# Hybrid decoder layer: the second pair of the up-projection in plain fp32, B11's rounding in small steps, and the last chunk's weights split slab by slab

## The chip, the core and the metric

The kernel runs on one core of a Trainium2 chip. TensorE (PE) multiplies, VectorE (DVE) and ScalarE (ACT) prepare its operands and empty its PSUM banks, GpSimd (POOL) adds and issues some DMAs, SyncE (SP) issues the others. The metric is the device time of one execution, in microseconds (us), the median of 3 runs. The engines do not share a program: each runs its own queue in order and waits on semaphores of the others.

## What is computed

One inference step of a decoder layer, for a prompt of 512 tokens and 8 single sample tokens (520 columns). After three groups of mixing heads and their output projection comes the part that the change touches:

```python
def conv_ffn(h, w_up, conv_w, conv_b, w_down, prefix):
    u = jnp.matmul(h, w_up)                       # 2048 -> 2 * 5632
    up = jnp.concatenate([prefix, u], axis=1)
    c = conv_b
    for j in range(CONV_W):                       # causal depthwise, width 3
        c = c + conv_w[j] * up[:, j:j + T]
    gate, val = jnp.split(c, 2, axis=-1)
    y = jnp.matmul(jax.nn.gelu(gate) * val, w_down)   # 5632 -> 2048
...
x = x + jnp.matmul(mix, w_out)
y, conv_new = conv_ffn(rms_norm(x, norm2), w_up, conv_w, conv_b, w_down, conv_buf)
x = x + y                                         # then the final rms_norm
```

All inputs and outputs are fp32.

## The kernel before

**Two ways to multiply.** A *split* product cuts each operand into a rounded part (hi, `F32R`) and a remainder (lo) and adds hi·hi, hi·lo and lo·hi: three matmuls for each 128 rows. A weight split is one rounding on ScalarE (L935) and one subtraction on VectorE (L937); an activation split (`split_act`, L1320 and L1321) is two halves of each. A *plain* product feeds fp32 operands to TensorE as they are, and needs no split.

**Seven products.** The up-projection runs in 44 pairs of 128 output columns: chunk by chunk of 512, gate and value in turn. A pair is a 2 x 2 block product over two halves of the inner dimension and two halves of the 520 columns. Pair 0 (`as_is_units`, L1189) computes it with eight plain block products. Each later pair (`seven_units`) uses seven products of sums of blocks: activations b11, t1 to t4, b21, b22 are sums and differences of the normed activation's four blocks, weights s1 to s4 (`sum1` to `sum4`, L1056 to L1065) are sums of the slab's blocks. Each product is a *unit*; they add into five PSUM banks. `post7` reads the bank that t1's product is in (c22, L1132), and the unit b22 then adds onto that bank; `c12` (L1126) reads the result. The down-projection of the first eight chunks follows in two *groups* of eight pairs each, the first of them plain, the rest with seven products; chunks 8 to 10 are then multiplied by 256 columns at a time with plain splitting (`plain`, L973).

**What is plain so far.** In pair 1, the first pair with seven products, b11, b21 and b22 are plain (`mm_raw`, L1225) and t1 to t4 are split, in the order b11, t1, t2, t3, b21, t4, b22. In pair 2, and in the first two such pairs of each group, b11 alone is plain; from then on b11 is split too, by `prep_b11`: the rounding of the whole block on ScalarE (L1361), two remainders on VectorE (L1365), their two roundings on ScalarE (L1369). It is written ahead of pair 2's sixth unit, in a group ahead of the fourth unit of the second such pair (U2).

**What sets the order.** Units stand in one list. For unit k the program first writes the weight split of unit k + 2, then the steps in `pre` (loads, sums, activation splits), then the matmuls, then `post` (evacuations), then one step of each background generator in `bg` (convolution, loads). The split tiles hi and lo have three buffers each. Engines run what they get in this order.

**Activations of the second norm.** `prep_t1` to `prep_t4` build the normed blocks and their differences and split each right away, during pair 0 and pair 1. Operands live in 14 numbered slots (`slot`), several of which hold first the residual x, which is stored to `x2d` at the start of pair 0, and xg, which pair 0 reads.

**Last chunk.** Chunk 10 is multiplied in 13 slabs of 512 x 256 weights: three for all columns, then twice five for half of the columns. Each slab is two units of 128 columns, each with its own weight split. A finished pair's `finish` squares and scales it on ScalarE (L1545, L1548), adds squares on GpSimd (L1546), transposes on TensorE (L1561) and copies on both (L1564); evacuation is L1479 on VectorE.

Of the kernel before, what the change touches and what calls it, by code (L numbers as in the profile page):

```python
# [17 lines left out]
P = 128  # L18
# [50 lines left out]
def hybrid_step(ctx: ExitStack, tc: tile.TileContext, I: dict, C: dict, O: dict):  # L69
# [862 lines left out]
    def split(view):  # L932
        nk = view.shape[1]
        hi = wp.tile([P, nk, P], F32R, tag="hi", name="hi", bufs=3)
        S.activation(hi, view, AF.Copy)  # L935
        lo = wp.tile([P, nk, P], F32R, tag="lo", name="lo", bufs=3)
        V.tensor_tensor(lo, view, hi.bitcast(F32), op=ALU.subtract)  # L937
        return hi, lo

    class Unit:  # L940


        def __init__(self, prod, mm, post=None):
            self.prod, self.mm, self.pre, self.post, self.w = prod, mm, [], post, None
# [6 lines left out]
    def plain(pairs_, src, act, load_at, cuts_of, evac, post):  # L951

        raws = {}
# [6 lines left out]
        def one(i, j):  # L960
# [17 lines left out]
            u = Unit(lambda: split(raws[i][:, :, j * P:(j + 1) * P]), mm, (lambda: post(i)) if j else None)  # L978
# [223 lines left out]
    def seven_units(p):  # L1202
# [55 lines left out]
        U = {4: Unit(lambda: split(A(p, 1, 1)), mm_split(4, "t4", True), post4),  # L1258
             5: Unit(lambda: split(SS[p, 1]), mm_split(3, "t1", True)),
             6: Unit(lambda: split(SS[p, 2]), mm_split(2, "t2", True), post6),  # L1260
             7: Unit(lambda: split(SS[p, 3]), mm_split(0, "t3", True), post7)}
# [392 lines left out]
```

## Time and profile before

| | us |
|---|---|
| median of 3 runs (lowest, highest) | 2308.23 (2307.58, 2309.12) |
| the profiled execution, its own time | 2307.24 |
| its span | 2305.2 |
| TensorE busy | 2255.0 (98%) |
| VectorE busy | 1591.7 (69%) |
| ScalarE busy | 955.0 (41%) |
| GpSimd busy | 200.9 (9%) |

The mean granted TensorE clock is 0.99 of full speed. The span is what lies between the first and the last instruction on the chip; the execution's own time is 2.0 us longer. Busy TensorE is matmuls with modelled ends. In rows, one plain matmul in the program is two records. The up-projection's pair 0 begins at 858 us, pair 1 at 888, the first group at 1780, the second at 1957, the last chunk at 2228.

### The profile page before, as it was taken

The numbers are of one execution on the slowest core, as the hardware profiler recorded it, in microseconds if no ns is written. First come the engines' busy times: TensorE is split into PE (matmuls) and PEld (weight loads), VectorE is DVE, ScalarE is ACT, GpSimd is POOL, SyncE is SP. The second block draws the span as 40 slices with busy tenths as digits, with TensorE's granted clock in tenths as the row PEclk, the third lists the DMA queues.
The fourth block names the chain that finished last, engine by engine and source line by source line (L and its number), as shares of the span: only waits on it lengthen the run. The fifth ranks groups of instructions, "written<-read, shape, count | busy, mean of one in ns | idle before, by whom it ended". The sixth has DMA issues, their size and how long they took to land.

```text
span 2305.2 us, 42433 instructions
## 1 busy us (share of the span) xinstructions
PE 2255.0 (98%) x18084; PEld 2221.7 (96%) x18084; DVE 1591.7 (69%) x2125; ACT 955.0 (41%) x1345; POOL 200.9 (9%) x424
## 2 busy tenths in 40 slices
PE   8999999999999999899999999999999999999996
PEld 8999999999999998899999999999999999999996
DVE  4365655444553448888888888988887977877446
ACT  6233332323342343544454454445444433434225
POOL 0001021121010110000000000000001001000002
PEclk9999999999999999999999999999999999999998
DMA  5323233334242442343433433343345446445514
GB/s 186 104 83 95 78 99 94 92 112 142 65 147 83 150 147 75 101 126 107 129 118 104 129 119 121 111 129 113 109 130 185 154 138 219 153 129 193 194 56 138
DMA packets 355020, 285.73 MB, mean 124 GB/s; under 512 B 9196, under 2 KB 336712, under 8 KB 353760
## 3 DMA queue, kind: packets, MB, share of 16 engines
q1 hardware_dynamic: 335728, 216.82, 31.2%
q0 software_dynamic: 19104, 66.21, 7.9%
q8 instruction: 142, 2.33, 0.4%
q14 instruction: 46, 0.38, 0.0%
HBM read 248.77 MB, written 36.64 MB: 124 GB/s over the span
## 4 chain that ended last, share of the span: by engine, by line
PE 71%; DVE 4%; ACT 1%; issue 1%; DMA 0%; ACTq 0%; DVEq 0%; POOLq 0%
PE pw L1218 16%; PE pw L1217 16%; PE pw L1219 16%; PE pw L973 9%; PE pg L186 3%; PE pg L190 3%; PE pg L188 3%; PE pw L1189 3%; DVE lo L937 1%; PE pw L1225 1%; ACT hi L935 1%; PE psc L703 1%; PE pob L685 1%; DVE n L1312 0%; PE px L750 0%
## 5 line engine op out<-in xcount | busy, mean ns | idle before, releaser
L935 ACT ACTIVATE hi<-r 128x1024 fp32r<-128x1024 f32 (+1 forms) x222 | 222.8, 1009 | 288.7 <-PE pw L1218 187.0
L937 DVE TENSOR_TENSOR lo<-s,hi 128x1024 fp32r<-128x1024 f32 x227 | 277.7, 1223 | 91.8 <-ACT hi L935 88.1
L935 ACT ACTIVATE hi<-s 128x1024 fp32r<-128x1024 f32 x227 | 240.0, 1058 | 187.0 <-PE pw L1218 174.4
L937 DVE TENSOR_TENSOR lo<-r,hi 128x1024 fp32r<-128x1024 f32 (+1 forms) x222 | 267.1, 1204 | 48.3 <-ACT hi L935 48.3
L186 PE MATMUL pg<-x1h,hi 128*128 128x260 f32 x1408 | 289.9, 287 | 3.0 <-ACT hi L157 1.7
L190 PE MATMUL pg<-x1h,lo 128*128 128x260 f32 x1408 | 284.4, 284 | 0.5 <-DVE lo L159 0.5
L188 PE MATMUL pg<-x1l,hi 128*128 128x260 f32 x1408 | 283.4, 283 | 0.0
L159 DVE TENSOR_TENSOR lo<-raw,hi 128x1024 fp32r<-128x1024 f32 x104 | 127.2, 1223 | 168.6 <-ACT hi L157 156.9
L186 PEld LDWEIGHTS pg<-x1h,hi 128*128 128x128 f32 x1408 | 217.8, 189 | 4.3 <-ACT hi L157 2.0
L190 PEld LDWEIGHTS pg<-x1h,lo 128*128 128x128 f32 x1408 | 217.5, 189 | 0.7 <-DVE lo L159 0.7
L188 PEld LDWEIGHTS pg<-x1l,hi 128*128 128x128 f32 x1408 | 217.1, 189 | 0.0
L1082 DVE SCALAR_TENSOR_TENSOR cv<-u,convc,cv 128x512 f32<-128x512 f32 (+1 forms) x176 | 132.2, 752 | 43.6 <-ACT cv L1077 43.6
L1217 PE MATMUL pw<-b22h,hi 128*128 128x260 f32 x448 | 129.1, 288 | 9.9 <-DVE cv L1145 7.8
L1217 PE MATMUL pw<-t1h,hi 128*128 128x260 f32 x456 | 130.2, 286 | 2.3 <-ACT hi L935 2.3
L1217 PE MATMUL pw<-t3h,hi 128*128 128x260 f32 x456 | 130.1, 285 | 2.3 <-ACT hi L935 2.3
L1219 PE MATMUL pw<-t3h,lo 128*128 128x260 f32 x456 | 130.1, 285 | 0.6 <-DVE lo L937 0.6
L1219 PE MATMUL pw<-t1h,lo 128*128 128x260 f32 x456 | 129.8, 285 | 0.7 <-DVE lo L937 0.7
L1217 PE MATMUL pw<-t4h,hi 128*128 128x260 f32 x456 | 130.3, 286 | 0.0
L1218 PE MATMUL pw<-t3l,hi 128*128 128x260 f32 x456 | 129.7, 284 | 0.0
L1219 PE MATMUL pw<-t4h,lo 128*128 128x260 f32 x456 | 129.1, 283 | 0.5 <-DVE lo L937 0.5
L1219 PE MATMUL pw<-t2h,lo 128*128 128x260 f32 x456 | 128.9, 283 | 0.6 <-DVE lo L937 0.6
L1218 PE MATMUL pw<-t1l,hi 128*128 128x260 f32 x456 | 129.4, 284 | 0.0
(442 smaller groups left out, 6357.1 us busy)
## 6 DMA issues: line engine op xcount, KB each, us to landing
r<-in_w_up SPq DMA_DIRECT2D x88, 1024.0 KB, 5.3
raw<-in_w_in SPq DMA_DIRECT2D x88, 512.0 KB, 3.6
r<-in_w_down SPq DMA_DIRECT2D x40, 1024.0 KB, 5.8
agd<-cv POOLq DMA_DIRECT2D x16, 520.0 KB, 3.7
g<-agd POOLq DMA_DIRECT2D x8, 1040.0 KB, 10.6
cv<-x2d POOLq DMA_DIRECT2D x16, 520.0 KB, 6.7
x2d<-cv POOLq DMA_DIRECT2D x16, 520.0 KB, 6.1
raw<-in_w_out SPq DMA_DIRECT2D x16, 512.0 KB, 3.3
```

The costliest lines, as they stand in the source:

```text
L159: V.tensor_tensor(lo, raw, hi.bitcast(F32), op=ALU.subtract)
L186: PE.matmul(ps[:, i, 0:b - a], wh, xh[:, a:b], start=first, stop=False)
L188: PE.matmul(ps[:, i, 0:b - a], wh, xl[:, a:b], start=False, stop=False)
L190: PE.matmul(ps[:, i, 0:b - a], wl, xh[:, a:b], start=False, stop=last)
L935: S.activation(hi, view, AF.Copy)
L937: V.tensor_tensor(lo, view, hi.bitcast(F32), op=ALU.subtract)
L973: PE.matmul(ps[t][:, 0:b - a], wt[:, kk], x[:, a:b], start=kk == 0 and wt is hi and x is xh, stop=kk == nk - 1 and wt is lo)
L1082: V.scalar_tensor_tensor(cv[:, j, 0:w], u[:, j, i:i + w], convc[:, i, n], cv[:, j, 0:w], op0=ALU.mult, op1=ALU.add)
L1189: PE.matmul(ps, A(p, n, i)[:, m], x[:, m], start=i == 0 and m == 0, stop=i == 1 and m == 7, skip_group_check=True)
L1217: PE.matmul(ps(k), hi[:, m], xh[:, m], start=a, stop=False, skip_group_check=True)
L1218: PE.matmul(ps(k), hi[:, m], xl[:, m], start=False, stop=False, skip_group_check=True)
L1219: PE.matmul(ps(k), lo[:, m], xh[:, m], start=False, stop=z, skip_group_check=True)
```

## The change

**Pair 1 wholly plain.** All seven units of pair 1 use `mm_raw`, in the order of the other pairs (b11, t4, t1, t2, t3, b21, b22), and no weight of pair 1 is split. Its second slab's successor is loaded from the third unit on.

**Activation splits put off.** Norms and differences come first, during pair 0, each block in a slot of its own; the splits of t1 and t2 come at the end of pair 0, of t3, t4 and b21 during pair 1, of b22 at the start of pair 2. Slots are renumbered for that.

**B11 in small steps.** `prep_b11` becomes a background generator of six steps, one behind each unit: rounding of each half, remainder of each half, rounding of each remainder. It starts ahead of pair 2's second unit, in a group ahead of U2's first.

**Last chunk.** A slab of the last chunk is split once, both units' columns in one instruction on each engine, and four units ahead instead of two.

```diff
-            u = Unit(lambda: split(raws[i][:, :, j * P:(j + 1) * P]), mm, (lambda: post(i)) if j else None)
+            def prod():
+                if not both:
+                    return split(raws[i][:, :, j * P:(j + 1) * P])
+                if j == 0:
+                    pieces[i] = split(raws[i])
+                return tuple(t[:, :, j * P:(j + 1) * P] for t in pieces[i])
+
+            u = Unit(prod, mm, (lambda: post(i)) if j else None)
+            u.ahead = 4 if both else 2
...
-        if p - 1 in as_is or p - 2 in as_is:
-            U[1] = Unit(None, mm_raw(1, lambda: A(p, 0, 0), (1, 1), True), post1)
-        else:
-            U[1] = Unit(lambda: split(A(p, 0, 0)), mm_split(1, "b11", True), post1)
-        if first:
-            U[2] = Unit(None, mm_raw(1, lambda: A(p, 0, 1), (2, 1), False), post2)
-            U[3] = Unit(None, mm_raw(3, lambda: SS[p, 2], (2, 2), False), post3)
-        else:
-            U[2] = Unit(lambda: split(A(p, 0, 1)), mm_split(1, "b21", False), post2)
-            U[3] = Unit(lambda: split(SS[p, 2]), mm_split(3, "b22", False), post3)
-        seq = (1, 5, 6, 7, 2, 4, 3) if first else (1, 4, 5, 6, 7, 2, 3)
-        at = [U[n] for n in seq]
-        at[3 if first else 2].pre.append(lambda: sum4(p))
+        def unit(k):
+            w, fresh = weights[k], k not in (2, 3)
+            if first or (k == 1 and p - 2 in as_is) or (k == 1 and p - 1 in as_is):
+                return Unit(None, mm_raw(banks[k], w, names[k], fresh), posts.get(k))
+            return Unit(lambda: split(w()), mm_split(banks[k], names[k], fresh), posts.get(k))
+
+        at = [unit(k) for k in (1, 4, 5, 6, 7, 2, 3)]
+        at[4 if first else 2].pre.append(lambda: sum4(p))
-            if first:
-                at[4].pre.append(lambda: load_pair(nx, 1))
-                at[6].pre.append(lambda: (sum1(nx), sum3(nx)))
-            else:
-                at[0].pre.append(lambda: load_pair(nx, 1))
-            if not first and nx not in as_is:
-                at[3].pre.append(lambda: sum1(nx))
-                at[4].pre.append(lambda: sum3(nx))
-                at[5].pre.append(lambda: sum2(nx))
+            at[2 if first else 0].pre.append(lambda: load_pair(nx, 1))
+            if nx not in as_is:
+                at[5 if first else 3].pre.append(lambda: sum1(nx))
+                at[6 if first else 4].pre.append(lambda: sum3(nx))
+                if not first:
+                    at[5].pre.append(lambda: sum2(nx))
...
     def prep_t1():
         norm2()
         B[1, 2] = normed(0, 1, 12)
-        B[1, 1] = normed(0, 0, 13)
-        B["t"] = slot(0, "t12", F32)
-        diff(B["t"], B[1, 2], B[1, 1])
-        xop["t1"] = split_act(B["t"], 1, 2, "t1")
+        B["b11"] = B[1, 1] = normed(0, 0, 13)
+        B["t1"] = slot(0, "t1", F32)
+        diff(B["t1"], B[1, 2], B[1, 1])
 
     def prep_t2():
-        B[2, 2] = normed(1, 1, 3)
-        diff(B["t"], B[2, 2], B["t"])
-        xop["t2"] = split_act(B["t"], 4, 5, "t2")
+        B["b22"] = normed(1, 1, 3)
+        B["t2"] = slot(1, "t2", F32)
+        diff(B["t2"], B["b22"], B["t1"])
+
+    def prep_t4():
+        B["b21"] = normed(1, 0, 2)
+        B["t4"] = slot(4, "t4", F32)
+        diff(B["t4"], B["t2"], B["b21"])
 
     def prep_t3():
-        diff(B[1, 2], B[2, 2], B[1, 2])
-        xop["t3"] = split_act(B[1, 2], 6, 7, "t3")
-
-    def prep_t4():
-        diff(B["t"], B["t"], B[2, 1])
-        xop["t4"] = split_act(B["t"], 9, 12, "t4")
+        B["t3"] = B[1, 2]
+        diff(B["t3"], B["b22"], B["t3"])
+
+    def split_b(name, h, l):
+        xop[name] = split_act(B[name], h, l, name)
 
     def prep_b11(h_, l_, tag, bufs):
 
         hi = slot(h_, "b11h")
-        S.activation(hi, B[1, 1], AF.Copy)
+        for a in (0, 4):
+            S.activation(hi[:, a:a + 4], B[1, 1][:, a:a + 4], AF.Copy)
+            yield
         halves = []
         for a in (0, 4):
             h = ff.tile([P, 4, HALF], F32R, tag=tag, name="b11x", bufs=bufs)
             V.tensor_tensor(h, B[1, 1][:, a:a + 4], hi[:, a:a + 4].bitcast(F32), op=ALU.subtract)
             halves.append(h)
+            yield
         lo = slot(l_, "b11l")
         for a, h in zip((0, 4), halves):
             S.activation(lo[:, a:a + 4], h.bitcast(F32), AF.Copy)
-        xop["b11"] = hi, lo
-
-    def split_b(i, t, name, h, l):
-        xop[name] = split_act(B[i, t], h, l, name)
-
-    def prep_n21():
-        B[2, 1] = normed(1, 0, 8)
+            xop["b11"] = hi, lo
+            yield
+
+    places = {"b11": (3, 13), "t4": (11, 0), "t1": (5, 6), "t2": (7, 8), "t3": (9, 10), "b21": (1, 12), "b22": (4, 2)}
+
+    def split_p(name, of=places):
+        split_b(name, *of[name])
 
     N, U1, U2 = ups[:3]
     N[0].pre.append(prep0)
     N[1].pre.append(prep_t1)
-    N[4].pre.append(prep_t2)
+    N[2].pre.append(prep_t2)
+    N[3].pre.append(prep_t4)
+    N[4].pre.append(prep_t3)
     N[5].pre += [lambda: sum1(1), lambda: sum2(1)]
-    U1[0].pre += [prep_t3, lambda: sum3(1)]
-    U1[2].pre += [prep_n21, prep_t4]
-    U1[6].pre.append(lambda: split_b(2, 1, "b21", 10, 11))
-    U2[0].pre.append(lambda: split_b(2, 2, "b22", 8, 0))
-    U2[5].pre.append(lambda: prep_b11(3, 13, "cv", 3))
+    N[6].pre += [lambda: sum3(1), lambda: split_p("t1")]
+    N[7].pre.append(lambda: split_p("t2"))
+    for k, u, name in ((0, U1, "t3"), (3, U1, "t4"), (5, U1, "b21"), (0, U2, "b22")):
+        u[k].pre.append(lambda name=name: split_p(name))
+    U2[1].pre.append(lambda: bg.append(prep_b11(3, 13, "cv", 3)))
...
-        U1[0].pre.append(lambda: split_b(2, 1, "b21", *new["b21"]))
-        U1[1].pre.append(lambda: split_b(2, 2, "b22", *new["b22"]))
-        U2[3].pre.append(lambda: prep_b11(*new["b11"], "u", 2))
+        U1[0].pre.append(lambda: split_b("b21", *new["b21"]))
+        U1[1].pre.append(lambda: split_b("b22", *new["b22"]))
+        U2[0].pre.append(lambda: bg.append(prep_b11(*new["b11"], "u", 2)))
...
+    made = 0
     for k, u in enumerate(units):
-        if k + 2 < len(units) and units[k + 2].prod:
-            units[k + 2].w = units[k + 2].prod()
+        while made < min(k + u.ahead + 1, len(units)):
+            if units[made].prod:
+                units[made].w = units[made].prod()
+            made += 1
```

Where B11's rounding stands on ScalarE. At the end of pair 2, before; b11h and b11l are its rounded part and its rounded remainder, b11x the remainder, r and s slabs and sums of weights, q the running sum, and L1077 the first tap of pair 2's convolution:

```order
L935 ACTIVATE hi<-r_9307 128x1024
L935 ACTIVATE hi<-s_9506 128x1024
L935 ACTIVATE hi<-r_9508 128x1024
L1361 ACTIVATE b11h<-n_9198 128x2080
L1369 ACTIVATE b11l<-b11x 128x1040 x2
L1123 COPY u<-pw_9518 128x260
L935 ACTIVATE hi<-r_9510 128x1024
L1077 ACTIVATE cv<-u,convc 128x512 x2
```

And after the change, at the same place on ScalarE:

```order
L934 ACTIVATE hi<-s_9428 128x1024
L1364 ACTIVATE b11h<-n_9198 128x1040
L934 ACTIVATE hi<-s_9407 128x1024
L1364 ACTIVATE b11h<-n_9198 128x1040
L934 ACTIVATE hi<-r_9310 128x1024
L934 ACTIVATE hi<-s_9428 128x1024
L934 ACTIVATE hi<-r_9430 128x1024
L1133 COPY u<-pw_9440 128x260
L1374 ACTIVATE b11l<-b11x 128x1040
L934 ACTIVATE hi<-r_9432 128x1024
L1087 ACTIVATE cv<-u,convc 128x512 x2
L1374 ACTIVATE b11l<-b11x 128x1040
```

The two halves of b11h moved ahead by two weight roundings and more, and the second half of b11l moved behind the convolution's first tap.

VectorE in the first group, in U2, before; cv is the residual that the sums are added to, the adds of q_19945 and pw_19847 are c22:

```order
L1065 TENSOR_TENSOR s_19734<-r_19578,s_19734 128x1024
L937 TENSOR_TENSOR lo<-r_19578,hi 128x1024
L1056 TENSOR_TENSOR s_19876<-r_19800 128x1024
L1365 TENSOR_TENSOR b11x<-g_19248,b11h 128x1040 x2
L1231 TENSOR_TENSOR q_19912<-q_19811,pw_19887 128x260
L937 TENSOR_TENSOR lo<-s_19734,hi 128x1024
L1059 TENSOR_TENSOR s_19918<-r_19798,r_19800 128x1024
L1231 TENSOR_TENSOR q_19945<-q_19912,pw_19920 128x260
L1145 TENSOR_TENSOR cv<-cv,q_19945 128x260
L1145 TENSOR_TENSOR cv<-cv,pw_19847 128x260
```

And after the change, at the same place on VectorE:

```order
L1075 TENSOR_TENSOR s_19657<-r_19501,s_19657 128x1024
L1369 TENSOR_TENSOR b11x<-g_19171,b11h 128x1040
L936 TENSOR_TENSOR lo<-r_19501,hi 128x1024
L1066 TENSOR_TENSOR s_19804<-r_19723 128x1024
L1241 TENSOR_TENSOR q_19831<-q_19734,pw_19806 128x260
L1369 TENSOR_TENSOR b11x<-g_19171,b11h 128x1040
L936 TENSOR_TENSOR lo<-s_19657,hi 128x1024
L1069 TENSOR_TENSOR s_19839<-r_19721,r_19723 128x1024
L1241 TENSOR_TENSOR q_19866<-q_19831,pw_19841 128x260
L1155 TENSOR_TENSOR cv<-cv,q_19866 128x260
```

The same instructions stand ahead of c22; one half of the remainder moved ahead of the weight remainder, the other behind q2.

VectorE in the last chunk, one half pair, before; x is the residual that is evacuated to, y the transposed output, u the scaled block:

```order
L937 TENSOR_TENSOR lo<-r_24060,hi 128x512
L1479 TENSOR_TENSOR x_22931<-pw_24171,x_22931 128x256
L937 TENSOR_TENSOR lo<-r_24060,hi 128x512
L1479 TENSOR_TENSOR x_22931<-pw_24189,x_22931 128x256
L1564 COPY y_23799<-py 128x256
L1547 TENSOR_SCALAR u<-x_22931,gv 128x256
```

And after the change:

```order
L936 TENSOR_TENSOR lo<-r_24027,hi 128x1024
L1485 TENSOR_TENSOR x_22856<-pw_24076,x_22856 128x256
L1485 TENSOR_TENSOR x_22856<-pw_24090,x_22856 128x256
L1570 COPY y_23724<-py 128x256
L1553 TENSOR_SCALAR u<-x_22856,gv 128x256
```

Two remainders of 512 became one of 1024, which stands ahead of both evacuations and belongs to a slab one pair further on.

## Rows read from the trace of the kernel before

**Rows 1.** Stretches: start:end, length; PE, PEld, DVE, ACT, POOL busy; clock, DMA share, GB/s.

```profile
858.00:880.00 22.00, 22.00 (x105) 19.13 (x104) 16.16 (x18) 6.33 (x11) 0.00 (x0) 1.00 0.49 150
...
920.00:960.00 40.00, 31.71 (x215) 30.48 (x214) 32.81 (x36) 19.68 (x22) 1.43 (x7) 0.87 0.32 98
...
960.00:1780.00 820.00, 820.00 (x6828) 820.00 (x6827) 721.63 (x829) 397.91 (x474) 54.48 (x185) 1.00 0.41 123
...
2260.00:2290.00 30.00, 25.55 (x200) 23.91 (x200) 22.74 (x52) 18.57 (x40) 7.91 (x6) 1.00 0.32 106
```

**Rows 2.** Chain that ended last: start, us, what.

```profile
788.09 5.79 PE pw L973 x48
...
1809.07 3.51 PE pw L1225 x16
```

**Rows 3.** Timeline, TensorE: start, us, line, out<-in, count, idle before and its releaser.

```profile
888.25 3.67 PE L1225 MATMUL pw<-n,r 128*128 128x260 f32 x16
...
943.24 0.36 PE L1217 MATMUL pw<-b22h,hi 128*128 128x260 f32 x1 [1.85 <-DVE u L1132]
...
950.43 0.38 PE L1217 MATMUL pw<-b11h,hi 128*128 128x260 f32 x1 [2.79 <-ACT u L1123]
...
954.94 0.28 PE L1217 MATMUL pw<-t4h,hi 128*128 128x260 f32 x1
...
1851.65 0.36 PE L1217 MATMUL pw<-b22h,hi 128*128 128x260 f32 x1 [3.92 <-DVE cv L1145]
...
1856.12 0.28 PE L1217 MATMUL pw<-b11h,hi 128*128 128x260 f32 x1
...
2027.75 0.56 PE L1217 MATMUL pw<-b22h,hi 128*128 128x260 f32 x1 [3.92 <-DVE cv L1145]
...
2033.08 0.42 PE L1217 MATMUL pw<-b11h,hi 128*128 128x260 f32 x1
...
2252.07 0.36 PE L973 MATMUL pw<-a10h,hi 128*128 128x256 f32 x1 [0.98 <-DVE x L1479]
```

**Rows 4.** Stretches of TensorE alone: start:end, length, busy (records), clock, DMA share, GB/s.

```profile
1851.60:1856.20 4.60, 4.55 (x25) 0.63 0.00 0
...
2027.70:2033.10 5.40, 5.35 (x25) 0.50 0.00 0
...
2252.10:2256.00 3.90, 3.50 (x29) 1.00 0.42 134
```

**Rows 5.** Timeline, VectorE, pairs 0 and 1.

```profile
867.96 4.70 DVE L1312 TENSOR_TENSOR n<-xg,rbc 128x1040 f32<-128x1040 f32 x4
...
887.64 1.22 DVE L937 TENSOR_TENSOR lo<-s,hi 128x1024 fp32r<-128x1024 f32 x1
```

**Rows 6.** Timeline, ScalarE, pair 2.

```profile
923.70 1.52 ACT L1077 ACTIVATE cv<-u,convc 128x512 f32<-128x512 f32 x2 [4.37 <-DVE u L1126]
...
925.12 1.04 ACT L935 ACTIVATE hi<-s 128x1024 fp32r<-128x1024 f32 x1
```

**Rows 7.** Timeline, VectorE, first group, U2.

```profile
1837.23 1.23 DVE L937 TENSOR_TENSOR lo<-s,hi 128x1024 fp32r<-128x1024 f32 x1 [1.26 <-ACT hi L935]
...
1847.89 1.23 DVE L937 TENSOR_TENSOR lo<-s,hi 128x1024 fp32r<-128x1024 f32 x1 [2.78 <-ACT hi L935]
```

**Rows 8.** Timeline, last chunk, one half pair on three engines; then TensorE's last pair.

```profile
2256.86 0.64 ACT L1545 ACTIVATE cv<-x 128x512 f32<-128x512 f32 x1 [0.86 <-DVE x L1479]
...
2257.64 1.29 POOL L1546 TENSOR_TENSOR cv<-cv 128x512 f32<-128x512 f32 x1 [2.68 <-ACT cv L1545]
...
2257.80 1.14 ACT L935 ACTIVATE hi<-r 128x512 fp32r<-128x512 f32 x2
...
2258.45 1.03 DVE L937 TENSOR_TENSOR lo<-r,hi 128x512 fp32r<-128x512 f32 x1 [1.08 <-ACT hi L935]
...
2259.74 0.68 DVE L937 TENSOR_TENSOR lo<-r,hi 128x512 fp32r<-128x512 f32 x1
...
2260.33 0.42 DVE L1479 TENSOR_TENSOR x<-pw,x 128x256 f32<-128x256 f32 x1
...
2285.48 0.36 PE L973 MATMUL pw<-a10h,hi 128*128 128x264 f32 x1 [1.48 <-DVE x L1479]
```

More of the change, by code (lines that the diff above doesn't have):

```diff
@@ L932, in split @@
     def split(view):
-        nk = view.shape[1]
-        hi = wp.tile([P, nk, P], F32R, tag="hi", name="hi", bufs=3)
+        hi = wp.tile(list(view.shape), F32R, tag="hi", name="hi", bufs=3)
         S.activation(hi, view, AF.Copy)
-        lo = wp.tile([P, nk, P], F32R, tag="lo", name="lo", bufs=3)
+        lo = wp.tile(list(view.shape), F32R, tag="lo", name="lo", bufs=3)
         V.tensor_tensor(lo, view, hi.bitcast(F32), op=ALU.subtract)
@@ L943, in __init__ @@
         def __init__(self, prod, mm, post=None):
-            self.prod, self.mm, self.pre, self.post, self.w = prod, mm, [], post, None
+            self.prod, self.mm, self.pre, self.post, self.w, self.ahead = prod, mm, [], post, None, 2
     units = []
@@ L951, in plain @@
     def plain(pairs_, src, act, load_at, cuts_of, evac, post):
-        raws = {}
+        raws, pieces = {}, {}
         def load(i):
@@ L976, in mm @@
                     evac(n0 + j, t, a, b, ps[t][:, 0:b - a])
-            u = Unit(lambda: split(raws[i][:, :, j * P:(j + 1) * P]), mm, (lambda: post(i)) if j else None)
+            both = nk == 4
+            def prod():
[6 more added lines that the diff above has]
+            u.ahead = 4 if both else 2
             if j == 0:
@@ L1242, in post7 @@
             out.c22(st["q3"], ps(3))
-            if not first:
-                out.c21(st["q3"], ps(4))
+            out.c21(st["q3"], ps(4))
         def post2():
             out.c11(ps(1))
-        def post4():
-            if first:
-                out.c21(st["q3"], ps(4))
         def post3():
@@ L1257, in seven_units @@
         nx = p + 1 if p + 1 < len(pairs) else None
[L1258 to L1261, printed above, removed]
-        if p - 1 in as_is or p - 2 in as_is:
-            U[1] = Unit(None, mm_raw(1, lambda: A(p, 0, 0), (1, 1), True), post1)
-        else:
-            U[1] = Unit(lambda: split(A(p, 0, 0)), mm_split(1, "b11", True), post1)
-        if first:
-            U[2] = Unit(None, mm_raw(1, lambda: A(p, 0, 1), (2, 1), False), post2)
-            U[3] = Unit(None, mm_raw(3, lambda: SS[p, 2], (2, 2), False), post3)
-        else:
-            U[2] = Unit(lambda: split(A(p, 0, 1)), mm_split(1, "b21", False), post2)
-            U[3] = Unit(lambda: split(SS[p, 2]), mm_split(3, "b22", False), post3)
-        seq = (1, 5, 6, 7, 2, 4, 3) if first else (1, 4, 5, 6, 7, 2, 3)
-        at = [U[n] for n in seq]
-        at[3 if first else 2].pre.append(lambda: sum4(p))
+        weights = {1: lambda: A(p, 0, 0), 2: lambda: A(p, 0, 1), 3: lambda: SS[p, 2], 4: lambda: A(p, 1, 1),
+                   5: lambda: SS[p, 1], 6: lambda: SS[p, 2], 7: lambda: SS[p, 3]}
+        names = {1: "b11", 2: "b21", 3: "b22", 4: "t4", 5: "t1", 6: "t2", 7: "t3"}
+        banks = {1: 1, 2: 1, 3: 3, 4: 4, 5: 3, 6: 2, 7: 0}
+        posts = {1: post1, 2: post2, 3: post3, 6: post6, 7: post7}
+        def unit(k):
[5 more added lines that the diff above has]
+        at[4 if first else 2].pre.append(lambda: sum4(p))
         if p == 2:
@@ L1394, in hybrid_step @@
     ORDER = ("b11", "t4", "t1", "t2", "t3", "b21", "b22")
-    places = {"b11": (3, 13), "t4": (9, 12), "t1": (1, 2), "t2": (4, 5), "t3": (6, 7), "b21": (10, 11), "b22": (8, 0)}
     def group(g, old):
@@ L1406, in load_b @@
         def load_b(i, t, s):
[L1407 removed]
+            B[i, t] = B[f"b{i}{t}"] = slot(s, f"g{i}{t}", F32)
             nc.gpsimd.dma_start(B[i, t], src[:, i - 1, :, HALF * (t - 1):HALF * t])
@@ L1609, in hybrid_step @@
         load_wo(i)
-    for u in units[:2]:
-        u.w = u.prod()
+    made = 0
     for k, u in enumerate(units):
-        if k + 2 < len(units) and units[k + 2].prod:
-            units[k + 2].w = units[k + 2].prod()
+        while made < min(k + u.ahead + 1, len(units)):
+            if units[made].prod:
+                units[made].w = units[made].prod()
+            made += 1
         for fn in u.pre:
```

2 lines of the change are left out of this document (removed).

## The prediction

> **What bounds the kernel now.** I read the table by stretch first, then the waits of TensorE, then what stands in front of them on VectorE and ScalarE. From 960 to 1780 us TensorE is busy for all 820 us at the full granted clock, and a stretch of plain fp32 matmuls (858 to 880) is also full [rows 1]. So only the places where it stops can give time. These are 920 to 960 (31.7 busy of 40, clock 0.87), one place in each of the two later groups, and the last 30 us of matmuls (25.6 busy) [rows 1]. The waits that matter for the end of the first place are 1.85 us before b22 of pair 2 and 2.79 before b11 of pair 3; each group has one of 3.92, before b22 of its second split pair [rows 3]. A wait also costs afterwards: the unit behind one of 3.92 us runs at 0.63 in the first group and 0.50 in the second, which is the 1.2 GHz level for most or all of it, and takes 4.47 and 5.33 us; after a wait of 0.98 us in the last chunk the clock stays at 1.00 [rows 3, 4].
>
> A split unit is 24 matmuls, half of a row with 48 in 5.79 us: 2.90. A plain unit is 8 matmuls, which the trace shows as 16 records: 3.51 [rows 2].
>
> **1, pairs 1 and 2 of the up-projection.** *On TensorE* pair 1 turns four split units into plain ones: 4 x (3.51 - 2.90) = +2.4 us. From 888.25 [rows 3], where pair 1 begins, pairs 1 and 2 then hold 8 plain and 6 split units, 28.1 + 17.4 = 45.5, so that pair 3 could begin at 933.7 and its second unit, t4, at 936.6, if nothing waited. That t4 begins at 954.94 now [rows 3]. The end of this term is the start of that t4, because from there no wait is left until the groups.
>
> The Trainium skill (FP8 and Floating Point Precision, TensorE Precision Notes) says that true FP32 takes four passes through the array. Against the three of a split matmul that would be 2.90 x 4/3 = 3.87 a unit, an estimate, and +3.9 us for four units; the row has 3.51 and decides, and the forecast would be 1.4 us higher by the page.
>
> *On VectorE* four remainder instructions of the weights of pair 1 go (1.22 us each, 1.13 from start to start [rows 5]), with four roundings on ScalarE; no wait of pair 1 is then for a split. I set the new order against durations. Pitches: half of an operand 1.15 (four take 4.70 to the end of the last [rows 5]), a 1024-wide instruction 1.13, a tap of the convolution 0.67, a 260-wide one 0.34. Differences and norms come first now: 867.96 + 16 halves (18.4) + two evacuations (0.7) = 887.1, then three sums to 890.5, t1's and t2's remainders with an evacuation behind each to 895.8. That last evacuation frees the bank of the third plain unit, which TensorE reaches at 888.25 + 7.0 = 895.3: a wait of about 0.7. Nothing else stops pair 1; its last sum (s4) is ready by 907, and TensorE needs it at 910. Pair 1 ends at 913.5, the plain unit of pair 2 at 917.0, its five split units at 931.5.
>
> The sixth, b22, adds onto the bank that holds t1's product, so it waits until c22 (L1132) has read it; the 1.85 us row is this wait [rows 3]. On VectorE there stand, between pair 1's last evacuations of the sums (907.6) and that c22: 6 halves (two each of b21 and b22, one of b11's remainder, and the gate product, which is as wide), 12 instructions of 1024, 4 taps, 3 short ones, c22 itself 0.9, and some 1.8 us in which it waits for ScalarE, whose Identity pair (1.52) stands before s1's rounding (1.04) [rows 6]: 6.9 + 13.6 + 2.7 + 1.0 + 0.9 + 1.8 = 26.9, so 934.5, and about 934.8 with what of the early wait comes through. So **the wait moves here**: b22 waits 3.3 us and then runs mostly at 1.2 GHz, 4.4 us (4.47 and 4.51 are what units behind such waits took [rows 3]), to 939.2. Next is b11's second low half. In the new order it stands on ScalarE behind the Identity pair of pair 2, which waits for c12, which waits for b22: 939.2 + c12 0.6 + 1.45 + 1.05 = 942.4. Pair 3's b11 has done its first 12 matmuls by then and does 12 more: t4 at 944.0. **Gain 954.9 - 944.0 = 10.9.** Bounds: none of these waits, 954.9 - 936.6 = 18.3; both with the longest waits and slowest clocks in the rows (3.92 + 5.33 for b22, 2.79 + 4.51 for b11, from 931.5: 948.1), 6.8.
>
> The DMAs of the next slabs move too: pair 2's second slab is now issued after pair 1's second unit (about 895), since its buffer's last reader comes earlier, and has over ten us until its sum is due at 908. ScalarE's table load and gelu stay where they were; they hide behind plain matmuls, and without that cover cost some 2.4 us once. The renamed slots cost nothing: the x2 stores that read slots 4 to 7 are issued at the start of pair 0, and the splits that reuse these slots come behind pair 0.
>
> **2, B11 in steps, twice in the groups.** Now the whole of b11's rounding (two halves as one instruction) and both low halves (2.04) stand on ScalarE before the rounding of s4, for which VectorE waits until 1847.89, and s3, q3 and c22 come behind [rows 7]. In the new order s4's rounding waits only for a free buffer, that is for t2, which ends at 1841.9. VectorE then goes without a wait from s3's remainder: that starts at 1837.23 [rows 7], 0.5 later with the first b11 step ahead of its rounding. Six of 1024 (6.8), two halves (2.3), q2 0.34, q3 and two adds 1.5: 1837.7 + 10.9 = 1848.6. The unit before b22 ends at 1847.56, so 1.1 us of the 3.92 stay. By the 0.98 us row the clock then holds, b22 ends at 1851.5, and b11 waits for the read of its bank, 3.42 us behind c22, until 1852.0. b11 starts at 1856.12 now: **4.1 us**. The second group has the same order and the same 3.92, but a slower unit behind it (b11 at 2033.08, 5.33 after b22's start at 2027.75): 5.0. **Together 9.1.** Bounds: all gone, 3.92 x 2 + 1.57 + 2.43 = 11.8; half of each wait stays and the clock still falls, 3.9.
>
> **3, last chunk.** One loop sets its pace, not TensorE: evacuation, then on ScalarE square, gain, rounding, then on VectorE remainder, next evacuation. The rows for one half pair: square from 2256.86, gain, two roundings 1.14, remainders 1.03 and 0.68, each with an evacuation of 0.34 to 0.42 [rows 8]; 3.97 us a turn. With one slab at once the second rounding no longer hides behind the first remainder: 0.08 + 0.54 + 0.40 + 1.06 + 1.14 + 0.34 + 0.42 = 3.98. No gain per turn. What is gained is the end: splitting two slabs ahead takes the last split off the last turn, where the last pair now waits until 2285.48 [rows 8]. Its predecessor's first bank can then be read at 2283.2, and behind its four transposes the pair starts at 2283.85: **1.6 us.**
>
> Here GpSimd matters: its add runs 2257.64 to 2258.93, and the remainder that starts at 2258.45 takes 1.03 where the next takes 0.68 [rows 8]. In the new order the remainder starts at 2258.9, as the add ends, so I charge nothing. The Trainium skill (SBUF, State Buffer; Who interferes with whom) says that an instruction of VectorE with two SBUF inputs blocks wholly against one of GpSimd that reads SBUF, the later one until the first has ended. By that rule, the trace agrees: 0.48 us of the add were left and 0.35 were lost. If the share were lost in each of 9 turns all the same, the term would be 1.6 - 9 x 0.35 = -1.5; at best the one 0.98 us wait at its start goes too: 2.6.
>
> **Sum.** 10.9 + 9.1 + 1.6 = 21.6 us. The profiled execution took 2307.24 us (span 2305.2 and 2.0 around it), 1.0 below the median of 2308.23. So 2285.6 for an execution like it, and in terms of the median 2286.6, said as 2287.
>
> **The rivals.**
> - *VectorE catches up* (each wait in 1 and 2 closes): 18.3 + 11.8 + 1.6 = 31.7, 2277. For it: VectorE loses four remainders and most of its waits. Against: c22 has 26 us of work before it with hardly a gap. Chance 0.12.
> - *The waits stay* at the lower bounds of 1 and 2 with nothing from 3: 6.8 + 3.9 = 10.7, 2297.5. For it: every wait over 1.8 us brought a slow unit. Against: by the count only 1.1 us is late in a group. Chance 0.15.
> - *The last chunk's halves were better* (the shared remainder in each turn): 2307.24 - 20.0 + 1.5, 2289.7 by the median. Chance 0.08.
> - *Slower, by the clock*: the new 0.7 us wait before pair 1's third unit drops the clock and it stays at 1.2 GHz. Every us of full-speed work costs another; from some 26 us on (21.6 to undo and 4.6 for 0.2%) the kernel is slower, and if it lasts from 895 to the end of pair 2 (38 us of work) the time is 2287 + 38 = 2325. Against: 0.98 us did not drop it, and after drops the rows show it back within a unit or two. Chance 0.03.
>
> **How the numbers follow.** The forecast has 0.62, alone from 2282 to 2292. A measurement of this kernel can tell about 0.2%, 4.6 us, from no change: faster is under 2303.6. The forecast, the first and the third rival lie there, and most of the second: 0.94. Within 0.2%: the far end of the second, 0.03. Slower: 0.03. The range leaves out about 0.1 on each side, the full first rival and the full second: 2280 to 2296.
>
> **What would show it.** Right: pair 1 as 56 plain matmuls without a wait over 1 us; a wait near 3 us for c22 before b22 of pair 2; one inside b11 of pair 3 for the second low half; waits near 1 us in the groups with the clock at 1.00; the last pair without a wait for a remainder. Wrong: a wait at pair 2's first split unit, a granted clock near 0.5 in pair 1, group waits still near 4 us, or a turn of the last chunk well off 4 us.

## The result, and the profile after

| | before | after |
|---|---|---|
| median, us (lowest, highest) | 2308.06 (2307.58, 2309.68), 6 runs | 2288.89 (2287.90, 2289.58), 6 runs |
| the profiled execution, its own time | 2307.24 | 2289.31 |
| its span | 2305.2 | 2287.5 |
| TensorE busy | 2255.0 (98%) | 2248.2 (98%) |
| VectorE busy | 1591.7 | 1581.8 |
| ScalarE busy | 955.0 | 949.5 |

The ratio is 0.9916 (95% interval 0.9903 to 0.9928): 19.2 us faster by the medians. The forecast was 2287, within 2280 to 2296.

By stretches of the kernel after (columns as in [rows 1]), the stretch that ends pair 2 has 33.7 us of matmuls in 40 where it had 31.7, and its clock is 0.96 where it was 0.87. The stretch from 2240 lies in the last chunk: 27.5 of 30. Earlier by the 17.7 us won in all, the last row there answers to 2242.3 to 2272.3 here, with 26.8 of 30 for its 25.6.

```profile
920.00:960.00 40.00, 33.66 (x263) 33.06 (x262) 34.54 (x40) 19.12 (x21) 1.09 (x5) 0.96 0.30 93
960.00:1780.00 820.00, 820.00 (x6798) 818.92 (x6797) 719.34 (x826) 397.11 (x474) 54.58 (x187) 1.00 0.41 123
2240.00:2270.00 30.00, 27.48 (x218) 26.07 (x219) 20.67 (x47) 18.69 (x35) 8.75 (x7) 1.00 0.29 97
```

TensorE's timeline of the kernel after, the rows that answer to [rows 3] and the two new waits (0.59 in pair 1, 0.92 in chunks 8 and 9):

```profile
896.11 2.24 PE L1235 MATMUL pw<-t,s 128*128 128x260 f32 x9 [0.59 <-DVE u L1130]
...
917.07 0.47 PE L1227 MATMUL pw<-t4h,hi 128*128 128x260 f32 x1
...
935.32 0.36 PE L1227 MATMUL pw<-b22h,hi 128*128 128x260 f32 x1 [2.99 <-DVE u L1142]
...
943.10 0.39 PE L1228 MATMUL pw<-b11l,hi 128*128 128x260 f32 x1 [3.12 <-ACT b11l L1374]
...
948.93 0.28 PE L1227 MATMUL pw<-t1h,hi 128*128 128x260 f32 x1
...
1840.19 0.36 PE L1227 MATMUL pw<-b22h,hi 128*128 128x260 f32 x1 [0.81 <-DVE cv L1155]
...
1843.59 0.36 PE L1227 MATMUL pw<-b11h,hi 128*128 128x260 f32 x1 [0.28 <-DVE cv L1155]
...
2012.24 0.36 PE L1227 MATMUL pw<-b22h,hi 128*128 128x260 f32 x1 [0.81 <-DVE cv L1155]
...
2131.06 0.63 PE L972 MATMUL pw<-a8h,hi 128*128 128x260 f32 x2 [0.92 <-ACT hi L934]
...
2236.23 0.38 PE L972 MATMUL pw<-a10h,hi 128*128 128x256 f32 x1 [1.39 <-DVE x L1485]
...
2267.77 0.37 PE L972 MATMUL pw<-a10h,hi 128*128 128x264 f32 x1
```

Since TensorE is the bound, the start of the same unit in both traces tells how much has been won up to there. Read so, the 17.7 us between the two spans come from these places:

| place | before | after | won so far | this part | forecast |
|---|---|---|---|---|---|
| pair 1, first unit | 888.25 | 888.35 | -0.1 | -0.1 | |
| pair 3, t1 | 957.82 | 948.93 | 8.9 | 9.0 | 10.9 |
| first group, t4 after b11 | 1859.01 | 1846.55 | 12.5 | 3.6 | 4.1 |
| second group, the same | 2036.15 | 2018.61 | 17.5 | 5.1 | 5.0 |
| chunks 8 and 9, to the last chunk's first transpose | 2239.74 | 2223.41 | 16.3 | -1.2 | |
| last chunk's last matmul, its end | 2288.64 | 2270.94 | 17.7 | 1.4 | 1.6 |

So the three terms came to 9.0, 8.7 and 1.4, and 1.2 us were lost where the forecast had nothing. The forecast for this execution was 2285.6, the measured 2289.3.

### The profile page after: what moved, and what is told of

Same layout as the page of the kernel before. It is cut to its first block, busy times and chain, and to the rows that moved or that the text cites. A ratio compares the mean times of both kernels' runs of the same rounds, so it can differ in the third digit from the quotient of the medians.

```text
span 2287.5 us, 42302 instructions
## 1 busy us (share of the span) xinstructions
PE 2248.2 (98%) x18052; PEld 2213.2 (97%) x18052; DVE 1581.8 (69%) x2108; ACT 949.5 (42%) x1331; POOL 200.4 (9%) x424
## 4 chain that ended last, share of the span: by engine, by line
PE 70%; DVE 5%; ACT 1%; issue 1%; DMA 1%; ACTq 0%; DVEq 0%; POOLq 0%
PE pw L1227 15%; PE pw L1228 15%; PE pw L1229 15%; PE pw L972 9%; PE pg L186 3%; PE pg L190 3%; PE pg L188 3%; PE pw L1199 2%; DVE lo L936 1%; PE pw L1235 1%; ACT hi L934 1%; DMA r<-in_w_down 1%; PE psc L703 1%; PE pob L685 1%; DVE t L1325 0%
## 5 line engine op out<-in xcount | busy, mean ns | idle before, releaser
L934 ACT ACTIVATE hi<-r 128x1024 fp32r<-128x1024 f32 x208 | 220.4, 1060 | 282.8 <-PE pw L1228 186.9
L936 DVE TENSOR_TENSOR lo<-r,hi 128x1024 fp32r<-128x1024 f32 x208 | 260.5, 1253 | 44.7 <-ACT hi L934 44.7
L1227 PE MATMUL pw<-b21h,hi 128*128 128x260 f32 x448 | 127.8, 285 | 0.0
L157 ACT ACTIVATE hi<-raw 128x1024 fp32r<-128x1024 f32 x104 | 109.6, 1056 | 43.1 <-PE pg L188 36.6
L1228 PE MATMUL pw<-t2l,hi 128*128 128x260 f32 x448 | 127.0, 283 | 0.0
L1228 PE MATMUL pw<-t4l,hi 128*128 128x260 f32 x448 | 126.9, 283 | 0.0
```

The lines of the kernel that those rows point to most:

```text
L157: S.activation(hi, raw, AF.Copy)
L1227: PE.matmul(ps(k), hi[:, m], xh[:, m], start=a, stop=False, skip_group_check=True)
L1228: PE.matmul(ps(k), hi[:, m], xl[:, m], start=False, stop=False, skip_group_check=True)
```

## Experiments

All medians below stand beside a kernel before of 2308.4 to 2308.8 us on the same chip.

**The kernel after once more** (no edit).

> The changed kernel itself once more. In its first profile pair 4 comes 9.0 us earlier than before, counted from pair 1's start; in four later kernels with the same program up to there it is 9.6, 10.5, 9.6 and 10.5. Theory: the length of pairs 2 and 3 differs from execution to execution, by which unit the low clock falls on and by how often b11 waits; this profile lies between 9.0 and 10.5, the time within 1.5 us of 2288.9. Rival: the first profile is the rule for this program, 9.0 again.

Measured: 2290.0 us (2287.22 to 2290.32), ratio 0.9916. Counted from pair 1's first unit to t2 of pair 3, the kernel before takes 72.48 us and the first profile of after 63.48, which is 9.0 less. This second profile has 61.99, which is 10.5 less. The five other kernels below that are the same up to there have 9.6 (twice) and 10.5 (three times). The difference is where the low clock falls and how long it lasts. In the second profile it falls on b22, right behind its wait, and is over before b11; in the two with 9.6 it lasts through b22 (0.50, 5.3 us) into b11. In the first it spares b22 and falls on t4, behind the next wait. Stretches of TensorE alone (columns as in [rows 4]), the first profile's b22, then its t4, then the second profile's b22:

```profile
935.30:938.30 3.00, 2.98 (x25) 1.00 0.00 0
...
944.80:949.00 4.20, 4.20 (x26) 0.66 0.01 2
```

```profile
936.30:940.70 4.40, 4.35 (x25) 0.67 0.00 0
```

**B11's split in the groups as before.**

```diff
-        U2[0].pre.append(lambda: bg.append(prep_b11(*new["b11"], "u", 2)))
+        U2[3].pre.append(lambda: list(prep_b11(*new["b11"], "u", 2)))
```

> The changed kernel with b11's split in the two groups at one go and in its old place, ahead of the fourth unit of the second split pair. Theory: it is this alone that moved the groups; the waits of 3.9 us before b22 come back with slow units behind them, and the time rises by what the starts of the units show, 3.5 + 5.2 = 8.7: 2297.6. Rival: part of the groups' gain came from work that reached them earlier or in another order from the pairs ahead; then the rise is under 6, below 2295.

Measured: 2298.9 us (2298.04 to 2299.32), 10.0 above after's first median, 8.9 above its second. The waits before b22 are back, at 3.85 (first group) and 3.86 us, and the units behind them last 4.4 and 4.5 us. The theory holds. TensorE in the first group:

```profile
1842.89 0.56 PE L1227 MATMUL pw<-b22h,hi 128*128 128x260 f32 x1 [3.85 <-DVE cv L1155]
```

**B11's split in the groups at one go, at its new place.**

```diff
-        U2[0].pre.append(lambda: bg.append(prep_b11(*new["b11"], "u", 2)))
+        U2[0].pre.append(lambda: list(prep_b11(*new["b11"], "u", 2)))
```

> The changed kernel with all six steps of b11's split in the groups written at once, at the place where the first of them stands now (ahead of the second split pair's first unit). Theory: what gave the groups' 8.7 us is the place, not the small steps; both remainders then stand where VectorE has nothing to do (3.73 us without work behind the plain unit), so the 0.81 and 0.28 us that are left in each group go too: 2288.9 - 2.2 = 2286.7. Rival: the steps matter, because ScalarE now stops for the plain unit's end (b11's remainder overwrites what that unit reads) with the weights' roundings behind it; a wait of TensorE of over 1 us comes in each group: 2291 or more.

Measured: 2286.97 us (2285.98 to 2287.28). TensorE waits nowhere in the first group now, and 0.24 us ahead of b11 in the second. Both remainders stand in VectorE's gap behind the plain unit, and ScalarE's stop for that unit's end held nobody up. What won the groups' 8.7 us is the place and not the small steps. Timelines of the first group, ScalarE and VectorE:

```profile
1825.03 2.04 ACT L1374 ACTIVATE b11l<-b11x 128x1040 fp32r<-128x1040 f32 x2 [4.37 <-DVE b11x L1369]
...
1822.55 2.38 DVE L1369 TENSOR_TENSOR b11x<-g,b11h 128x1040 fp32r<-128x1040 f32 x2
1828.32 2.36 DVE L936 TENSOR_TENSOR lo<-s,hi 128x1024 fp32r<-128x1024 f32 x2 [3.38 <-ACT hi L934]
```

**Pair 1's part alone.**

```diff
-    U2[1].pre.append(lambda: bg.append(prep_b11(3, 13, "cv", 3)))
+    U2[5].pre.append(lambda: list(prep_b11(3, 13, "cv", 3)))
...
-        U2[0].pre.append(lambda: bg.append(prep_b11(*new["b11"], "u", 2)))
+        U2[3].pre.append(lambda: list(prep_b11(*new["b11"], "u", 2)))
...
-                if not both:
+                if True:
...
-            u.ahead = 4 if both else 2
+            u.ahead = 2
```

> Only the change in pair 1 (plain units, splits put off): b11's split in pair 2 and in the groups is at one go in its old place, and the last chunk is split as before. Theory: the 8.9 us by which pair 3's t1 came forward belong to pair 1's part alone; c22 has one remainder less ahead of it (b22 waits 1.8 and not 3.0), and b11's split is late instead: 2308.4 - 8.9 = 2299.5. Rival: the small steps carry a good part of it; b11's split of 6.3 us in a row stands behind c22 and holds b11 of pair 3 up by over 4 us: 2303 or more.

Measured: 2299.34 us (2298.85 to 2302.25), 9.5 under the kernel before. b22 waits 1.80 and b11 2.69, about the 1.85 and 2.79 of [rows 3], with a clock of 0.65 and 0.63 behind them. From pair 1's first unit to t2 of pair 3 it takes 63.23 us, 9.25 less than before, where the seven profiles with the small steps have 9.0 to 10.5. So nearly all of the first term is pair 1's: the small steps in pair 2 traded a shorter wait at b11 for a longer one before b22, and were worth between -0.3 and 1.3 us, as far as one profile of this kernel tells.

```profile
935.46 0.36 PE L1227 MATMUL pw<-b22h,hi 128*128 128x260 f32 x1 [1.80 <-DVE u L1142]
...
942.59 0.39 PE L1227 MATMUL pw<-b11h,hi 128*128 128x260 f32 x1 [2.69 <-ACT u L1133]
```

**B11's last two steps as one, in pair 2.**

```diff
             xop["b11"] = hi, lo
-            yield
+            if a == 4 or not together:
+                yield
```

(`together` is set for pair 2 only.)

> The changed kernel with the last two steps of b11's split in pair 2 made one: both roundings of the remainders stand together on ScalarE, ahead of the convolution's Identity pair. Theory: the 3.12 us wait inside b11 of pair 3 is this place in ScalarE's queue and nothing else, and the slow t4 behind it (4.2 at a clock of 0.66) comes from the wait; both go, t1 of pair 3 starts at 944.1 instead of 948.9, 2284.1. Rival 1: the wait of 2.99 us before b22 drops the clock by itself; then 3.1 is gained, 2285.8. Rival 2: the weight rounding that now stands behind both is late for t4, which waits 1 us instead: 2285.1 at best.

Measured: 2286.53 us (2285.26 to 2289.93). The wait inside b11 is gone: both halves of b11l stand ahead of the Identity pair. But the rounding of t1's weights now stands behind that pair too, and t1, begun at 944.27 (expected 944.1), waits 0.75 inside the unit for the remainder made from it and ends 4.1 us after its start, at a clock of 1.00. This is the second rival, one unit later than it said. In this execution a wait of 2.96 before b22 did not lower the clock at all, so it cannot tell how much of the slow t4 came from which wait. ScalarE, then TensorE, then TensorE's stretch that holds t1:

```profile
936.95 2.04 ACT L1374 ACTIVATE b11l<-b11x 128x1040 fp32r<-128x1040 f32 x2 [3.97 <-DVE b11x L1369]
...
941.70 1.52 ACT L1087 ACTIVATE cv<-u,convc 128x512 f32<-128x512 f32 x2 [1.76 <-DVE u L1136]
943.13 1.04 ACT L934 ACTIVATE hi<-s 128x1024 fp32r<-128x1024 f32 x1
...
945.48 0.40 PE L1229 MATMUL pw<-t1h,lo 128*128 128x260 f32 x1 [0.75 <-DVE lo L936]
```

```profile
944.40:948.30 3.90, 3.15 (x26) 1.00 0.43 129
```

**The same, and pair 1's gate product behind c22.**

```diff
+        if p == 1:
+            yield
         V.tensor_tensor(cv, GT[c, o], cv, op=ALU.mult)
```

> The changed kernel with both remainder roundings of b11 in one step, as in the run before, and pair 1's gate product one step later, that is behind c22 on VectorE. Theory: b22 of pair 2 waits for nothing but the instructions queued ahead of c22 on VectorE; with one of 1.15 us less the wait falls from 2.96 to 1.8, and what is won is lost again in front of b11, because the remainder of its weights still ends at 937.8: 2286.0, 0.5 less than with the one step alone (2286.5). Of the clock: a wait of 1.8 us is still followed by a slow unit. Rival 1: c22 waits for its bank or for ScalarE; then b22's wait stays at 3 and the time at 2286.5. Rival 2: the wait of 1.8 leaves the clock at 1.00: 2285 or less.

Measured: 2286.80 us (2286.64 to 2287.41). b22 waits 1.83 us where it waited 2.96: 1.13 less for one instruction of 1.15 less on VectorE. So the queue ahead of c22 is the wait. The clock behind it is 0.63, b11 has no wait, and the time is that of the run before. The theory is right on b22's wait and on the slow unit behind it. It is wrong on where the gain is lost: not in front of b11, but in b22 itself, which takes 4.5 us where it took 3.0 in the run before.

```profile
935.56 0.36 PE L1229 MATMUL pw<-b22h,hi 128*128 128x260 f32 x1 [1.83 <-DVE u L1144]
```

**The last chunk split as before.**

```diff
-                if not both:
+                if True:
...
-            u.ahead = 4 if both else 2
+            u.ahead = 2
```

> The changed kernel (2288.9 us) with the last chunk's weight split as it was before: each unit's 128 columns by themselves, two units ahead. Theory, from the two traces: the split by slabs gained 1.93 us at the last pair and lost 0.4 where the full slabs end, while the 1.2 us lost at the start of chunks 8 and 9 (VectorE waits 8.91 for a residual's load, TensorE 0.92) has nothing to do with it. Then 2288.9 + 1.5 = 2290.4, and the wait of about 0.9 in chunks 8 and 9 stays. Rival: the new split caused that wait too; then it is gone and the time is 2288.9 + 0.3 = 2289.2.

Measured: 2291.53 us (2290.41 to 2292.35), 2.6 above after's first median and 1.5 above its second. The wait in chunks 8 and 9 stays and is 1.58 here, so the new split is not its cause. From the first transpose of the last chunk to the end of its last matmul this kernel takes 48.9 us, like the kernel before and the one with pair 1 alone; the kernel after (twice) and five others with its last chunk take 47.3 to 47.6. The split is worth 1.4 us.

**The last chunk split three units ahead.**

```diff
-            u.ahead = 4 if both else 2
+            u.ahead = 3 if both else 2
```

> The changed kernel with the last chunk's slabs split three units ahead instead of four, so that on VectorE the remainder stands behind the first of the two evacuations of a pair and not ahead of both. Theory: the turn of 3.98 us is the chain square, gain, rounding, remainder, two evacuations; with one evacuation out of it, it is 3.6, TensorE's own 3.7 (a pair of 3.1 and 0.6 of transposes) becomes the bound, and 9 turns give 9 x 0.27 = 2.4: 2286.5. Rival: the first evacuation waits for its bank anyway, the remainder is pushed back by as much, and the turn stays: 2288.9.

Measured: 2286.30 us (2285.42 to 2286.65). The last chunk takes 44.8 us from first transpose to last matmul, 2.7 less. In the kernel after a turn is 3.98 us, from one square on ScalarE to the next, as forecast; here it is 3.67. From the first transpose to the last matmul TensorE waits three times, 1.3 us in all, where it waited seven times, 4.1 us. First the kernel after, then this one:

```profile
2236.60 0.63 ACT L1551 ACTIVATE cv<-x 128x512 f32<-128x512 f32 x1 [1.35 <-DVE x L1485]
...
2240.58 0.63 ACT L1551 ACTIVATE cv<-x 128x512 f32<-128x512 f32 x1 [0.40 <-DVE x L1485]
```

```profile
2238.52 0.64 ACT L1551 ACTIVATE cv<-x 128x512 f32<-128x512 f32 x1 [1.15 <-DVE x L1485]
...
2242.19 0.63 ACT L1551 ACTIVATE cv<-x 128x512 f32<-128x512 f32 x1 [1.17 <-DVE x L1485]
```

**The first residual of chunks 8 and 9 loaded earlier.**

```diff
-    down_units[0].pre += [lambda: load_x2(0), lambda: load_x2(1)]
+    last[6].pre.append(lambda: load_x2(0))
+    down_units[0].pre.append(lambda: load_x2(1))
```

> The changed kernel with the first residual of chunks 8 and 9 loaded one unit earlier, ahead of the last store of the groups, in the same queue. Theory: the 1.2 us lost at the start of chunks 8 and 9 is this load, which lands 7.9 to 9.6 us after the last sum of the groups and is late from about 8 us on; loaded earlier it is never late, the wait of 0.9 us before the second a8 unit goes, 2287.7. Rival: the wait is for the bank or the weights and not for the load: 2288.9.

Measured: 2286.78 us (2286.63 to 2288.40), and no wait at that place. The 2.1 below after's first median are more than the wait was; the execution that was profiled also has the 10.5 us of above and not the 9.0. VectorE's first evacuation of these chunks waits for the load, issued behind the groups' last store. Where VectorE's idle time there is 7.70 (before) or 7.88 (the run with three units ahead) TensorE does not wait; where it is 8.91 (after) it waits 0.92, and with 9.58 (the last chunk as before) 1.58. In all ten profiles with the load at its old place TensorE's wait is what this idle time has above 8.0 us: 0.34 at 8.34, 1.72 at 9.71. The profile of the kernel after names a rounding on ScalarE as the last releaser of its 0.92; in the seven others that wait it is this evacuation. Loaded earlier, VectorE's first evacuation is ready at 2123.21, not 2130.48, and waits for TensorE alone. The kernel after, GpSimd and VectorE; then this kernel, VectorE:

```profile
2121.26 1.05 POOL L1481 DMA_DIRECT2D x<-x2d  x2
...
2130.48 0.76 DVE L1485 TENSOR_TENSOR x<-pw,x 128x260 f32<-128x260 f32 x2 [8.91 <-DMA x<-x2d]
```

```profile
2123.21 0.76 DVE L1485 TENSOR_TENSOR x<-pw,x 128x260 f32<-128x260 f32 x2 [2.72 <-PE pw L972]
```

**Four edits together:** b11's last two steps as one in pair 2, its split at one go in the groups, three units ahead in the last chunk, the early load.

> The changed kernel with four edits of the runs before together: b11's two remainder roundings in pair 2 in one step, its split in the groups at one go at its present first place, the last chunk split three units ahead, the first residual loaded earlier. Theory: they act at four different places and add up: 2288.9 - 2.4 - 1.9 - 2.4 - 1.2 = 2281.0. Rival: two of them remove the same delay, or the load, now early, makes others late; then 2284 or more.

Measured: 2281.37 us (2279.65 to 2282.16), ratio to the kernel before 0.9880 (0.9865 to 0.9895). They add up as expected, within the spread of the runs.

**The four, and c22 earlier.** Pair 1's gate product one step later as above, and

```diff
-                at[6 if first else 4].pre.append(lambda: sum3(nx))
+                at[6 if first or p == 2 else 4].pre.append(lambda: sum3(nx))
```

> As the run with four edits, and in pair 2 pair 1's gate product and pair 3's sum s3 behind c22 on VectorE, 2.3 us of work. Theory: b22's wait falls from 3.0 to 0.7 us, after which the clock holds as it did after 0.98 us; b11 then waits some 0.6 for the remainder of its weights, which ends 1.15 earlier; 2.2 for the waits and 1.3 for the slow unit: 2281.0 - 3.5 = 2277.5. Rival: the wait moves whole to b11's weights, and the clock falls there: 2280 or more.

Measured: 2279.30 us (2278.45 to 2281.40), ratio 0.9874 (0.9858 to 0.9891), the fastest here; its lead on the run before is not clear of the spread of either. The first two waits are what was expected, 0.69 and 0.60, and the clock stays at 1.00. But t1 of pair 3 waits 1.15 for its weights' rounding, which stands behind the Identity pair on ScalarE, and 0.75 for the remainder. Together that is 1.9 us, about the 1.8 by which the expected 2277.5 is missed.

```profile
932.64 0.36 PE L1229 MATMUL pw<-b22h,hi 128*128 128x260 f32 x1 [0.69 <-DVE u L1144]
...
936.46 0.39 PE L1230 MATMUL pw<-b11l,hi 128*128 128x260 f32 x1 [0.60 <-ACT b11l L1376]
...
943.68 0.39 PE L1229 MATMUL pw<-t1h,hi 128*128 128x260 f32 x1 [1.15 <-ACT hi L934]
```

## Why the prediction was right, point by point

**Pair 1, plain.** Right. The eight plain units, pair 1's seven and the first of pair 2, run from 888.35 to 917.07, which is 3.52 each without the wait at 896.11; forecast were 3.51, a wait of 0.7 (found 0.59) and 917.0. The Trainium skill (FP8 and Floating Point Precision, TensorE Precision Notes), with its four passes for true FP32, would have made a unit 3.87 by the estimate in the prediction; the measured 3.52 speaks against taking passes alone for the time.

That longer units win here comes mainly from two waits that the prediction does not price by themselves. In the kernel before, TensorE waits for a rounding on ScalarE ahead of t3 of pair 1 and of t1 of pair 2, and these units take 6.2 and 5.5 us, at a mean clock of 0.52 and 0.69. In the kernel after both waits are gone, and b22 of pair 2 starts 46.97 us behind pair 1's first unit, not 54.99. TensorE before:

```profile
900.00 0.41 PE L1217 MATMUL pw<-t3h,hi 128*128 128x260 f32 x1 [2.30 <-ACT hi L935]
...
926.21 0.39 PE L1217 MATMUL pw<-t1h,hi 128*128 128x260 f32 x1 [2.35 <-ACT hi L935]
```

**The wait that moves to b22.** Right in mechanism, place and size: c22 on VectorE was forecast for 934.5 and starts at 934.75, b22's wait was forecast as 3.3 and is 2.99. The run with the product later shows that this wait is the queue ahead of c22. The slow b22 that was forecast behind it came in seven of the nine profiles with this wait, but not in the first of the kernel after.

**The wait inside b11.** Right in place: ScalarE's second half of b11l stands behind the Identity pair, which waits for c12. It was forecast to end at 942.4, and TensorE goes on at 943.10. In the first profile b22 ran at full clock and c12 could have come early, but on VectorE it stood behind four instructions of 1.2 us that reach to 939.98, which the forecast's "c12 0.6" left out. So it is partly luck that the forecast end is only 0.7 off: b22 ended 0.8 earlier than forecast, and c12 began 1.6 behind its end, where the forecast had it right behind. Timelines of the kernel after, VectorE and ScalarE:

```profile
938.85 1.22 DVE L936 TENSOR_TENSOR lo<-r,hi 128x1024 fp32r<-128x1024 f32 x1
939.98 0.41 DVE L1136 TENSOR_TENSOR u<-q,pw 128x260 f32<-128x260 f32 x1
...
940.57 1.52 ACT L1087 ACTIVATE cv<-u,convc 128x512 f32<-128x512 f32 x2 [1.80 <-DVE u L1136]
941.99 1.05 ACT L1374 ACTIVATE b11l<-b11x 128x1040 fp32r<-128x1040 f32 x1
```

**Where term 1 was mis-sized.** t4 of pair 3 starts at 944.76, forecast 944.0. The step that failed is the sentence that ends the term there because no wait is left behind it. None is, but the low clock can come behind the last wait as well: in the first profile t4 itself ran at 0.66 and cost 1.3 more, beside the 0.8 by which it began late. In executions where b22 gets the low clock, as the forecast had it, t4 is fast and the term is 10.5, or 9.6 where the low clock lasts into b11; 10.9 was a little above all seven.

**The groups.** 8.7 for 9.1. The wait left before b22 was forecast as 1.1 and is 0.81, the clock behind it stays at 1.00 as forecast, and b11 waits 0.28 where 0.5 was forecast. The first group gave 3.6 and not 4.1, since its first split pair waited 0.32 for c22, behind a slab for which VectorE had waited 0.56; six of the eleven other profiles with pair 1 plain have such a wait. The second group gave 5.1, forecast 5.0.

**The last chunk.** 1.4 for 1.6, by two effects that the forecast had only one of. No gain per turn, as forecast, and the last pair starts without a wait. It is 1.9 us closer to the pair ahead of it than before: at 2267.77 its lead on the kernel before is 17.71 us, and that of the pair ahead of it 15.78. But 0.4 was lost on the way in: the first half pair waits 1.39 where it waited 0.98, because its evacuation now stands behind the whole remainder, which beside GpSimd's add takes 1.48 us. The rival about better halves expected a loss in each turn from the remainder beside GpSimd's add; six of the eight remainders from 2234 on take 1.22 to 1.23 us, the other two 1.42 and 1.48, and the turn is as forecast. What the run three units ahead shows instead is that the place of the remainder among the evacuations set the pace.

**What was not in the forecast.** The 1.2 us in chunks 8 and 9: the residual's load takes 7.9 us from issue to landing in the kernel before, just in time, and 8.1 to 9.9 in the nine later profiles with the load at this place, of which eight have the wait. In the second profile of the kernel after it was 1.72. The change edits nothing there. Whether the profile of before was lucky or the load is slower now stays open: there is one profile of the kernel before.

**The rivals.** VectorE did not catch up (2277): c22 was late as counted. The waits did not stay at their lower bounds (2297.5). The clock did not stay low through pairs 1 and 2 (2325): behind 0.59 us it did not fall. The third rival's 2289.7 lies nearer to the measured 2288.9 than the forecast does, but for another reason: the last chunk gained 1.4 us and did not lose 1.5.

**Left open.** How much of term 1 is the plain units and how much the splits that were put off: the two share slots of memory and were not tried apart. What would remove the last waits of t1 in the fastest kernel was not tried either.

## What to carry to other kernels

When a step is put off or cut up, write down the queue of each engine around the place where it lands, with durations, up to the next unit of the bound engine that reads from it; here that gave the waits that were forecast, or their ends, to within 0.7 us; it did not give the low clock, the landed loads or the first wait of the last chunk. Count the instructions ahead of every link of the chain, short ones like c12 too. Before cutting a step into small ones, try it whole at the same early place: in the groups the place was everything, and the whole step there was better.

## What the runs showed of the hardware

- A wait of 2.96 to 3.01 us ahead of b22 of pair 2 stands in nine profiles whose code is the same up to there. In seven it brought the low clock onto b22 (0.50 to 0.67, 4.3 to 5.3 us), in two not (1.00, 2.9 us); in one of these the low clock then came on t4, behind a wait of 3.12, in the other not at all.
- Shorter waits of 1.80, 1.83 and 1.85 us ahead of b22 also brought it (0.65, 0.63, 0.66), and 0.69 and 0.81 us did not. Nor did 1.58 and 1.72 us in chunks 8 and 9, or 1.79 us inside b11 in the second profile of the kernel after. These waits stand at different places, so this is a list and no threshold.
- One load behind a store in the same queue landed between 7.9 and 9.9 us after its issue, in ten profiles; a transfer with no slack can therefore cost nothing in one execution and 1.7 us in another.
- VectorE's remainder of 128x1024 took 1.48 us at 2234.36, beside the last 0.4 us of GpSimd's add, and 1.23 at 2242.60, practically without it.
